# Attention scores one pair ahead, feed-forward pieces in traced order, other buffers for the first raw weights

## The chip, the cores and the metric

The kernel runs on one core of one Trainium2 chip. The metric is the time of one execution on the device in microseconds, as the median of several runs.

## What is computed

One layer of an encoder over two groups of tokens with the same weights: x_prompt (1024 tokens) and x_sample (512 tokens), width 1024, all float32. With DEPTH = 1 only the neighbourhood attention of the reference is used:

```python
def run(x):
    h = rms_norm(x, norm_mix[0])
    x = x + neighbourhood_attention(h, na_w_qkv[0], na_rpb[0], na_w_o[0])
    x = x + swiglu(rms_norm(x, norm_ffn[0]), ffn_w_gate[0], ffn_w_up[0], ffn_w_down[0])
    return rms_norm(x, norm_final)
```

Tokens lie on a grid 64 columns wide. There are 16 heads of width 64; 16 query columns look at a band of 32 key columns in 8 rows, with a learned bias and a mask. swiglu has a hidden width of 2816 and is (silu(x w_gate) * (x w_up)) w_down.

## The kernel before

A float32 product is made of three fp32r products on TensorE (PE): each operand is split into a high part (a CAST on ACT) and a low part (a subtraction on DVE, or for a few on POOL), and hi*hi, hi*lo and lo*hi are added up in PSUM. `split` (L139 to L145) does this for weights and activations.

The work comes in stages. (1) Norms, transposes and the V projection of all tokens (L250 to L324). (2) Attention of the prompt, by head pair hp = 0 to 7. A head pair has four steps (two halves g of the query rows, two pairs jj of column blocks), and `step` (L477) traces one: the scores of the pair's two blocks u = 0, 1 (`pss`, L397, with the bias addition and row maximum on DVE L405, Exp on ACT L408, reciprocal L410, scaling L412 on DVE for one head and L414 on ACT for the other), then the weighting (`po`, L434) and the collection (L444 to L447) of the pair before, then the flips, that is PE transposes (`ptt`, L423), of its own scores into `pT` (split on ACT L426, DVE L427). Between these stand fillers: `fill(part)` takes 6 matmuls (`pg`, L335) at a time of the q and k projection of the next head pair. Scores and flips take turns in four PSUM banks (tag "S"). (3) The same for the sample with two key tiles, beside the output projection (`pgo`, L593). (4) The feed-forward gate and up products, by Strassen's scheme of seven half-size products, for two chunks c of 768 tokens. `unit(c, p)` (L865) makes block p = 0 to 10 (256 columns) of gate and up: 14 products of 12 matmuls (L824), evicted by ACT (COPY, Silu) and DVE, followed by four sums on POOL (`gs`, L884 to L887) and seven stores of down operands to gop_d (L889). `w_ops` (L787) loads raw weights through `w_raw` (L779), whose counter `turn` deals them to two buffers of rpool and three of r2p (the right side of memory, where the attention's `wo` lay before), and splits them. (5) The down products (L1062).

Units of stage 4 take other work along: `tick` (L906) is called after each of the 14 products and takes one piece of a generator at every second call. In the first chunk, p = 1 to 10, these are the norm, transposes and operand sums of the second chunk (`pair1`, 42 pieces, three token groups); in the second chunk, p = 3 to 10, the sums of rows of w_down (`down_sums`, 56 pieces for 11 blocks, each with two subtractions on DVE L768, L770 and two on POOL L773, L775, two loads and two stores).

A scheduler sets the order in which each engine's instructions stand: it may move an instruction ahead of what was traced before it if no data forbids. Each engine and each DMA queue (SP's, ACT's, POOL's) then works strictly in that order. Only where the code records a manual dependency, as `in_order` (L98) does for the start, is the traced order kept.

## Time and profile before

| | |
|---|---|
| median of 3 runs | 1808.15 us (1807.66 to 1812.14) |
| the profiled execution | 1815.71 us, span 1813.8 us |
| PE busy | 1749.2 us (96%) |
| DVE busy | 1215.9 us (67%) |
| ACT busy | 870.6 us (48%) |
| POOL busy | 431.2 us (24%) |
| DMA engines, mean over the span | 163 GB/s |
| granted clock of TensorE, mean | 0.992 |

Busy time is the time in which an engine executes instructions; the rest of the span it waits or has nothing to do. PE is the engine that works nearly all the time, so the place of its waits matters, and what each of the other engines does just before.

### The profile page before, as it was taken

The numbers are of one execution on the slowest core, as the hardware profiler recorded it, in microseconds if no ns is written. First come the engines' busy times: TensorE is split into PE (matmuls) and PEld (weight loads), VectorE is DVE, ScalarE is ACT, GpSimd is POOL, SyncE is SP. The second block draws the span as 40 slices with busy tenths as digits, with TensorE's granted clock in tenths as the row PEclk, the third lists the DMA queues.
The fourth block names the chain that finished last, engine by engine and source line by source line (L and its number), as shares of the span: only waits on it lengthen the run. The fifth ranks groups of instructions, "written<-read, shape, count | busy, mean of one in ns | idle before, by whom it ended". The sixth has DMA issues, their size and how long they took to land.

```text
span 1813.8 us, 25894 instructions
## 1 busy us (share of the span) xinstructions
PE 1749.2 (96%) x9178; PEld 1527.3 (84%) x9178; DVE 1215.9 (67%) x2267; ACT 870.6 (48%) x1742; POOL 431.2 (24%) x509
## 2 busy tenths in 40 slices
PE   7999999999999999999999999989999999999998
PEld 6888777777777788779999999888999987888886
DVE  4401878788787666667877777988777756446553
ACT  4411777667785555544444445433344335433423
POOL 1111000000130000112424242565424352005300
PEclk9999999999999999999999999999999999999999
DMA  7755333333464453653553634888433269555633
GB/s 237 224 182 168 98 107 109 108 103 106 131 204 149 135 157 111 193 181 119 177 171 111 216 109 146 284 298 275 137 115 122 75 210 324 180 158 165 206 110 107
DMA packets 229858, 295.60 MB, mean 163 GB/s; under 512 B 27648, under 2 KB 173824, under 8 KB 229728
## 3 DMA queue, kind: packets, MB, share of 16 engines
q1 hardware_dynamic: 205744, 215.94, 39.3%
q0 software_dynamic: 21248, 69.62, 10.5%
q10 hardware_dynamic: 2736, 8.39, 1.5%
q8 instruction: 72, 1.18, 0.3%
q14 instruction: 58, 0.48, 0.1%
HBM read 218.45 MB, written 87.97 MB: 169 GB/s over the span
## 4 chain that ended last, share of the span: by engine, by line
PE 69%; DMA 11%; DVE 9%; ACT 4%; issue 4%; SPq 2%; POOL 2%; DVEq 0%; ACTq 0%; POOLq 0%
PE pa L824 16%; PE pd L1062 16%; PE pd L824 8%; PE pg L335 7%; PE pgv L281 7%; DMA vr<-v_d 5%; PE pgo L593 4%; PE pb L824 4%; PE pss L397 3%; SPq L381 2%; PE po L434 1%; PE ptt L423 1%; DMA gr<-gop_d 1%; DMA wt_d<-t 1%; ACT s L408 1%
## 5 line engine op out<-in xcount | busy, mean ns | idle before, releaser
L1062 PE MATMUL pd<-wd,go 128*128 128x512 f32 x1386 | 325.7, 396 | 3.6 <-DVE wd L142 2.6
L1062 PEld LDWEIGHTS pd<-wd,go 128*128 128x128 f32 x1386 | 260.4, 188 | 68.8 <-DVE wd L142 4.9
L824 PE MATMUL pa<-h,ws 128*128 128x384 f32 x1056 | 199.4, 336 | 8.7 <-ACT c L849 7.2
L335 PE MATMUL pg<-hTp,whl 128*128 128x512 f32 x768 | 201.9, 407 | 0.0
L824 PE MATMUL pd<-h,ws 128*128 128x384 f32 x1056 | 197.6, 334 | 0.0
L824 PEld LDWEIGHTS pa<-h,ws 128*128 128x128 f32 x1056 | 183.1, 188 | 12.0 <-ACT c L849 9.2
L824 PEld LDWEIGHTS pd<-h,ws 128*128 128x128 f32 x1056 | 184.3, 188 | 0.0
L142 DVE TENSOR_TENSOR ws<-wt,ws 128x1024 fp32r<-128x1024 f32 x88 | 109.9, 1250 | 90.9 <-ACT ws L141 90.9
L335 PEld LDWEIGHTS pg<-hTp,whl 128*128 128x128 f32 x768 | 139.2, 190 | 34.2 <-issue 7.7
L824 PE MATMUL pa<-h,wa 128*128 128x384 f32 x792 | 151.1, 343 | 8.3 <-DVE c L856 8.3
L824 PEld LDWEIGHTS pa<-h,wa 128*128 128x128 f32 x792 | 141.4, 191 | 10.5 <-DVE c L856 10.5
L593 PE MATMUL pgo<-wo,oh 128*128 128x512 f32 x576 | 139.0, 392 | 1.4 <-DVE oh L142 1.4
L141 ACT CAST go<-gr 128x768 fp32r<-128x768 f32 x84 | 65.7, 782 | 151.6 <-PE pd L1062 106.7
L408 ACT ACTIVATE s<-s,mx 128x384 f32<-128x384 f32 (+1 forms) x192 | 109.1, 570 | 54.8 <-DVE mx L405 54.8
L142 DVE TENSOR_TENSOR wa<-wr,wa 128x512 fp32r<-128x512 f32 x132 | 124.0, 952 | 13.1 <-ACT wa L141 12.1
L142 DVE TENSOR_TENSOR go<-gr,go 128x768 fp32r<-128x768 f32 x84 | 81.6, 972 | 75.0 <-ACT go L141 73.4
L593 PEld LDWEIGHTS pgo<-wo,oh 128*128 128x128 f32 x576 | 107.4, 188 | 24.4 <-DVE oh L142 1.8
L889 POOL DMA_DIRECT2D gop_d<-c x66 | 50.6, 766 | 313.1 <-DVE c L880 313.1
L141 ACT CAST wa<-wr 128x512 fp32r<-128x512 f32 x132 | 81.8, 621 | 88.5 <-PE pb L824 43.5
L141 ACT CAST ws<-wt 128x1024 fp32r<-128x1024 f32 x88 | 92.4, 1051 | 63.3 <-issue 49.7
L335 PE MATMUL pg<-hTs,whl 128*128 128x512 f32 x384 | 105.7, 411 | 2.0 <-DVE q L346 2.0
L824 PE MATMUL pb<-h,wa 128*128 128x384 f32 x528 | 101.0, 339 | 4.3 <-ACT wa L141 4.1
(158 smaller groups left out, 2945.3 us busy)
## 6 DMA issues: line engine op xcount, KB each, us to landing
wr<-ffn_w_gate SPq DMA_DIRECT2D x44, 512.0 KB
wr<-ffn_w_up SPq DMA_DIRECT2D x44, 512.0 KB
wr<-na_w_qkv SPq DMA_DIRECT2D x38, 512.0 KB
gop_d<-gs POOLq DMA_DIRECT2D x88, 192.0 KB, 5.7
gr<-gop_d SPq DMA_DIRECT2D x42, 384.0 KB
gr<-gop_d SPq DMA_DIRECT2D x42, 320.0 KB
gop_d<-c POOLq DMA_DIRECT2D x66, 192.0 KB, 2.5
vr<-v_d SPq DMA_DIRECT2D x192, 64.0 KB
```

Source lines behind the costliest of these rows:

```text
L141: nc.scalar.copy(hi, raw)
L142: nc.vector.tensor_tensor(lo, raw, f32(hi), ALU.subtract)
L281: nc.tensor.matmul(pg, hh[a][:, k, c:c + P], wv[k // 2][b][:, k % 2], start=(k == 0 and i == 0), stop=(k == KB - 1 and i == 2))
L335: nc.tensor.matmul(pg, w[:, a, k, :], h[b][:, k, c:c + 512], start=(k == 0 and i == 0), stop=(k == KB - 1 and i == 2))
L381: nc.sync.dma_start(out=raw[:, j * P:(j + 1) * P], in_=src[:, BS[j]:BS[j] + 32, :])
L397: nc.tensor.matmul(pt[:, :n], q[h * HD:(h + 1) * HD, a, j].rearrange("p r i -> p (r i)"), kv[:, krow:krow + nrow, BS[j]:BS[j] + 32], start ...
L408: nc.scalar.activation(s[:, :n], s[:, :n], AF.Exp, bias=mx, scale=-1.0, accum_out=sm)
L423: nc.tensor.transpose(pt[:, c * P:(c + 1) * P], s[:, c * P:(c + 1) * P], ident)
L593: nc.tensor.matmul(pg, ohs[k // 4][:, a, k % 4], wo[:, b, k, n * 512:(n + 1) * 512], start=(k == 0 and i == 0), stop=(k == KB - 1 and i == 2))
L824: nc.tensor.matmul(bank[:, :HT], a(y, k), b[:, z, k], start=start and k == 0 and i == 0, stop=k == KB // 2 - 1 and i == 2, skip_group_chec ...
L889: nc.gpsimd.dma_start(out=gop_d[i, 3 * c:3 * c + 3, :, p].rearrange("j q t -> q j t"), in_=a.rearrange("q (j t) -> q j t", j=3))
L1062: nc.tensor.matmul(pd, go[:, y, i - a], wds[m, i][:, z], start=(i == 0 and k == 0), stop=(i == NP - 1 and k == 2))
```

## The change

Four edits. In attention, `step` keeps the softmax tiles `ss` of the pair instead of its flipped `pT`, and flips them in the next step, ahead of their weighting; `fill` is called four times with one piece each; the tiles s have six buffers instead of four, tmp and oT one instead of two. In the feed-forward stage a piece's instructions on ACT, DVE, POOL and SP are chained in the order in which they are traced, behind the last instruction traced before it on the same engine (`pinned`). The counter `turn` starts at 4, so the first two raw halves go to rpool and the next three to r2p. The tile `edge`, at the very end of memory, has 224 bytes a partition instead of 96, which moves all pools of the right side by 128 bytes, to addresses that are multiples of 256; those of the left side in stages 2 to 4 already are.

```diff
-        edge = es.enter_context(tc.tile_pool(name="edge", bufs=1, side="right")).tile([P, 24], F32, name="edge")
+        edge = es.enter_context(tc.tile_pool(name="edge", bufs=1, side="right")).tile([P, 56], F32, name="edge")
...
+        def pinned(work, *engines):
+
+            traced = nc.cur_bb.bb.instructions
+            mark = traced[-1]
+            done = next(work, 0) == 0
+            start = next(k for k in reversed(range(len(traced))) if traced[k] is mark) + 1
+            for e in engines:
+                own = [i for i in traced[start:] if i.engine == e.engine]
+                if own:
+                    last = next((i for i in reversed(traced[:start]) if i.engine == e.engine), None)
+                    for a, b in zip([last] + own, own):
+                        if a is not None:
+                            tc.add_manual_dep(b, a.name, mybir.DependencyInfo(
+                                mybir.DependencyClass.NoSync, mybir.DependencyReason.DATA), reason="pinned")
+            return done
...
-                s = ap.tile([P, 384], F32, tag="s", name="s", bufs=4)
+                s = ap.tile([P, 384], F32, tag="s", name="s", bufs=6)
...
         def collect(pos, dst):
+            tmp = ap.tile([P, 2, P], F32, tag="tmp", name="tmp", bufs=1)
             for h in range(2):
...
-                tmp = ap.tile([P, 2, P], F32, tag="tmp", name="tmp")
...
-            oT = ap.tile([P, 512], F32, tag="o", name="oT", bufs=2)
+            oT = ap.tile([P, 512], F32, tag="o", name="oT", bufs=1)
...
             fill(0)
             if prev:
-                p, pT = prev.pop()
+                p, pss = prev.pop()
+                pT = []
+                for u, x in enumerate(pss):
+                    pT.append(flip(x, p["n"]))
+                    fill(1 + u)
                 pos = [psum("V", "po") for _ in range(2)]
                 for u in range(2):
                     weighted(pT[u], [x() for x in p["v"]], p["jj"] * 2 + u, p["n"], pos, u)
                 collect(pos, p["dst"])
                 if p["done"]:
                     p["done"]()
-            pT = []
-            for u, x in enumerate(ss):
-                pT.append(flip(x, st["n"]))
-                fill(1 + u)
+            else:
+                fill(1)
+                fill(2)
+            fill(3)
             if st:
-                prev.append((st, pT))
+                prev.append((st, ss))
...
-                run(fillers, 1 if part or last else 2)
+                run(fillers, 0 if last and part % 2 else 1)
...
-                run(fillers, 1 if part else 2)
-                run(ofill, 1 if part else 2)
+                run(fillers, 1)
+                run(ofill, 1)
...
-        turn = [0]
+        turn = [4]
...
-                    next(work, None)
+                    pinned(work, nc.scalar, nc.vector, nc.gpsimd, nc.sync)
```

Line numbers in the rows below are those of each kernel; up to 20 lines lie between the two (L405 before is L421 after, L773 is L793).

Place 1, a step of the prompt's attention on DVE (s: softmax tile, mx: row maximum, ri: reciprocal of the row sum, pT: flipped tile, tmp and oT: collected output). Before:

```order
L405 ISA s,mx<-pss,bp 128x384
L405 ISA mx 128x1
L410 RECIPROCAL ri<-sm 128x1
L405 ISA s,mx<-pss,bp 128x384
L405 ISA mx 128x1
L412 TENSOR_SCALAR s<-s,ri 128x384
L410 RECIPROCAL ri<-sm 128x1 x2
L412 TENSOR_SCALAR s<-s,ri 128x384
L410 RECIPROCAL ri<-sm 128x1
L445 TENSOR_TENSOR tmp<-tmp,po 64x256 x2
L447 TENSOR_TENSOR oT<-tmp,po 64x2x8x16 x2
L427 TENSOR_TENSOR pT<-ptt,pT 128x3x128 x4
```

and after:

```order
L421 ISA s,mx<-pss,bp 128x384
L421 ISA mx 128x1
L426 RECIPROCAL ri<-sm 128x1
L421 ISA s,mx<-pss,bp 128x384
L421 ISA mx 128x1
L428 TENSOR_SCALAR s<-s,ri 128x384
L426 RECIPROCAL ri<-sm 128x1 x2
L428 TENSOR_SCALAR s<-s,ri 128x384
L426 RECIPROCAL ri<-sm 128x1
L443 TENSOR_TENSOR pT<-ptt,pT 128x3x128 x4
L461 TENSOR_TENSOR tmp<-tmp,po 64x256
L463 TENSOR_TENSOR oT<-tmp,po 64x2x8x16
```

The four subtractions of pT stood behind the collection and belonged to the scores above them; now they stand ahead of the collection and belong to the pair before, which is the pair that is collected.

Place 2, ACT at the change from attention's output to unit 0 of the first chunk (oh: output operand, wa and ws: split weights, wr: raw weights, t<-x_d: loads for the second chunk's norm). Before:

```order
L141 CAST oh<-wr 128x512
L141 CAST wa<-wr 128x512
L676 DMA t_9327<-x_d 128x1024
L676 DMA t_9328<-x_d 128x1024
L141 CAST wa<-wr 128x512 x2
L842 COPY c<-pa 128x384
L680 ACTIVATE t_9325,ms<-t_9327 128x1024
L141 CAST wa<-wr 128x512
L141 CAST ws<-wt 128x1024 x2
L141 CAST wa<-wr 128x512 x2
```

and after:

```order
L157 CAST oh<-wr 128x512
L157 CAST wa<-wr 128x512 x2
L157 CAST ws<-wt 128x1024 x2
L157 CAST wa<-wr 128x512 x2
L862 COPY c<-pa 128x384
L157 CAST wa<-wr 128x512
L896 ACT_TABLE_LOAD
L896 ACTIVATE c<-c 128x384
```

All splits of the first gate block but its last stand ahead of the first eviction now, and the first norm loads of the second chunk have gone some 15 rows down.

Place 3, POOL in the second chunk (t: sums of rows of w_down, gs: sums of a unit, gop_d: stores of a unit). Before:

```order
L889 DMA gop_d<-gs 128x3x128 x4
L773 TENSOR_TENSOR t_13224<-t_13224,t_13223 128x512
L775 TENSOR_TENSOR t_13224<-t_13224 128x512
L773 TENSOR_TENSOR t_13448<-t_13448,t_13447 128x512
L775 TENSOR_TENSOR t_13448<-t_13448 128x512
L773 TENSOR_TENSOR t_13638<-t_13638,t_13637 128x512
L775 TENSOR_TENSOR t_13638<-t_13638 128x512
L889 DMA gop_d<-c 128x3x128 x2
L884 TENSOR_TENSOR gs<-c 128x384
```

and after:

```order
L909 DMA gop_d<-gs 128x3x128 x4
L795 TENSOR_TENSOR t_13176<-t_13176 128x512
L793 TENSOR_TENSOR t_13400<-t_13400,t_13399 128x512
L795 TENSOR_TENSOR t_13400<-t_13400 128x512
L909 DMA gop_d<-c 128x3x128 x2
L904 TENSOR_TENSOR gs<-c 128x384
L905 TENSOR_TENSOR gs<-gs,c 128x384
L906 TENSOR_TENSOR gs<-c 128x384
L907 TENSOR_TENSOR gs<-c,gs 128x384
L909 DMA gop_d<-c 128x3x128
L909 DMA gop_d<-gs 128x3x128 x4
L793 TENSOR_TENSOR t_13590<-t_13590,t_13589 128x512
```

Before, two or three row blocks of the sums stand between the sums of two units, and all 11 are done in the first units of the chunk; now one or two stand there, spread over eight units to the chunk's last.

## Rows read from the trace of the kernel before

**Rows 1.** The page, engines: busy time, share of the span, instructions.

```profile
PE 1749.2 (96%) x9178; PEld 1527.3 (84%) x9178; DVE 1215.9 (67%) x2267; ACT 870.6 (48%) x1742; POOL 431.2 (24%) x509
```

**Rows 2.** Waits of PE from 230 to 580: total us, times, longest.

```profile
PE pss L397 <- DVE pT L427: 5.5, 7, 0.9
PE ptt L423 <- ACT s L414: 5.2, 12, 1.4
PE ptt L423 <- DVE s L412: 4.8, 5, 1.4
PE pg L335 <- DVE q L346: 2.0, 1, 2.0
```

**Rows 3.** Timeline of PE, one head pair: start, duration, instructions [idle before].

```profile
330.80 2.19 PE L397 MATMUL pss<-kp,q 64*128 64x384 f32 x12 [0.86 <-DVE pT L427]
...
352.54 1.52 PE L397 MATMUL pss<-kp,q 64*128 64x384 f32 x12
...
373.66 1.37 PE L397 MATMUL pss<-kp,q 64*128 64x384 f32 x7 [0.84 <-DVE pT L427]
```

**Rows 4.** Windows: length, busy PE, PEld, DVE, ACT, POOL, clock, DMA, GB/s.

```profile
300.00:400.00 100.00, 95.86 (x561) 76.97 (x560) 78.57 (x228) 69.44 (x173) 7.58 (x19) 1.00 0.35 102
```

**Rows 5.** Windows of units: 0; 1 to 6; 11 to 14; 16 to 20.

```profile
797.40:833.50 36.10, 31.82 (x170) 30.99 (x169) 25.14 (x39) 20.30 (x31) 3.20 (x5) 0.91 0.55 176
833.50:1018.80 185.30, 181.37 (x1057) 179.98 (x1057) 145.78 (x199) 82.61 (x134) 65.46 (x70) 1.00 0.53 166
...
1136.10:1271.80 135.70, 122.63 (x673) 119.21 (x672) 122.37 (x143) 50.65 (x84) 78.80 (x66) 0.98 0.84 286
...
1301.50:1448.00 146.50, 146.50 (x842) 146.14 (x842) 107.47 (x141) 60.72 (x100) 52.41 (x55) 1.00 0.35 109
```

**Rows 6.** Timelines of SP, ACT and PE at the start of unit 0.

```profile
785.61 0.38 SPq L784 DMA_DIRECT2D wr<-ffn_w_gate  x1
...
797.64 0.38 SPq L784 DMA_DIRECT2D wr<-ffn_w_gate  x1
...
803.06 1.14 ACT L141 CAST wa<-wr 128x512 fp32r<-128x512 f32 x2 [17.93 <-DMA wr<-ffn_w_gate]
...
803.74 1.01 PE L824 MATMUL pb<-h,wa 128*128 128x384 f32 x2 [4.06 <-ACT wa L141]
```

**Rows 7.** Windows of low granted clock (seventh value), as in rows 4.

```profile
801.70:808.60 6.90, 4.65 (x13) 4.14 (x14) 4.97 (x8) 4.74 (x8) 0.00 (x0) 0.51 1.04 356
1235.20:1238.70 3.50, 3.50 (x11) 3.50 (x12) 3.50 (x6) 0.00 (x0) 0.78 (x1) 0.51 0.97 341
```

**Rows 8.** Timelines of PE, DVE and POOL in the second chunk.

```profile
1178.76 2.38 PE L824 MATMUL pa<-h,ws 128*128 128x384 f32 x12 [2.03 <-ACT c L849]
...
1178.91 2.89 DVE L768 TENSOR_TENSOR t<-t 128x512 f32<-128x512 f32 x1
...
1179.95 1.30 POOL L773 TENSOR_TENSOR t<-t,t 128x512 f32<-128x512 f32 x1
...
1192.98 0.69 DVE L768 TENSOR_TENSOR t<-t 128x512 f32<-128x512 f32 x1 [1.43 <-DMA t<-ffn_w_down]
```

**Rows 9.** Waits of PE from 800 to 1130, first chunk.

```profile
PE pa L824 <- ACT c L849: 3.9, 2, 2.4
```

**Rows 10.** Timelines of SP and PE at the start of the down stage.

```profile
1464.95 0.34 SPq L1000 DMA_DIRECT2D gr<-gop_d  x1
...
1481.02 5.34 PE L1062 MATMUL pd<-wd,go 128*128 128x512 f32 x14 [2.38 <-DVE wd L142]
```

**Rows 11.** Groups by shape: count, busy us, mean ns, idle before.

```profile
L335 PE MATMUL pg<-hTp,whl 128*128 128x512 f32 x768 | 201.9, 407 | 0.0
...
L335 PE MATMUL pg<-hTs,whl 128*128 128x512 f32 x384 | 105.7, 411 | 2.0 <-DVE q L346 2.0
```

**Rows 12.** Groups by shape, DVE: the bias addition and its maximum.

```profile
L405 DVE CUSTOM_DVE_ANT_0 s<-pss,bp 128x384 f32<-128x384 f32 x128 | 65.4, 547 | 1.2 <-PE pss L397 1.1
...
L405 DVE DVE_READ_ACCUMULATOR2_ANT mx<- 128x1 f32 x192 | 15.8, 83 | 0.0
```

## The prediction

> **What bounds the kernel now.** I read the shares of the engines first: PE is busy 1749.2 us of the span, 96% [rows 1], so a gain can only come out of PE's waits, of stretches in which its clock is low, and of waits too short for the list. Then the waits of PE by stage, and for the feed-forward stage the windows unit by unit, because there each unit holds the same work (14 products of 12 matmuls) and its length can be compared.
>
> Attention of the prompt: in 350 us PE waits 17.5 us for four things [rows 2], nearly all of it at two places of a step: the first scores (pss) wait for a score bank that the last split of a pT must free, and the flips (ptt) wait for the softmax (s, from ACT L414 or DVE L412). In the timeline of one head pair the step takes 42.86 us from scores to scores (330.80 to 373.66); the scores that start after a wait take 2.19 us and the unhindered ones 1.52 [rows 3]. DVE is not far behind PE there: 78.6 of 100 us [rows 4].
>
> Feed-forward: five units without extra pieces take 146.5 us, so 29.3 each, with PE never idle, although POOL works 52.4 us beside DVE in them [rows 5]. Unit 0 takes 36.1, the six units with the norm pieces 185.3 (9.5 more than six times 29.3), and the first four units of the second chunk 135.7 (18.5 more than 117.2). That last stretch is also where DVE is busy 122.4 of 135.7. These 34.8 us are the larger part of what can be had.
>
> **The change, part by part.**
>
> *First raw weights.* Unit 0's second raw half is loaded only at 797.64 [rows 6], after the last pgo (797.4, where the first window of rows 5 begins): its buffer lies where wo still was. ACT waits 17.93 us for it, and PE stands 4.06 us before the second product [rows 6]. The granted clock is then low (0.51, the 1.2 GHz level) from 801.7 to 808.6 [rows 7]. With the new start of the counter both halves of w_gate's first block go to rpool, whose second buffer could be loaded at 785.61 already [rows 6], some 12 us before it is needed; w_up's two halves then take the late place, and its first product comes seven products after 797.4, 14.6 us later by the unit's 29.3, against 5.4 us from issue (797.64) to ACT (803.06) [rows 6]. In the new order ACT splits both before the first COPY (place 2 of the order). So the unit loses its 6.8 us of excess; I take 6.3. Ends: 4.1 if the clock still falls, 6.8 if all goes, and nothing if a load meets another wait.
>
> *Pieces in traced order.* 56 pieces of down_sums stood, by the scheduler's choice, in the first four units of the second chunk; now 7 stand in each of eight units, p = 3 to 10 (place 3 of the order). The work stays. What is saved is the crowding: in those units a subtraction of DVE takes 2.89 us while POOL runs its own, and 0.69 alone, and PE waits 2.03 us for a COPY that ACT has queued behind a Silu that waits for DVE [rows 8]. Price of a piece in uncrowded units: the 42 norm pieces cost 9.5 us, 0.23 each, PE's own transposes in that; their named PE waits alone are 3.9 us [rows 9], 0.09 each. So 56 pieces cost 5.2 to 12.9 us; I take 7, nearer the lower end because these pieces put nothing on PE or ACT, and leave 1 us for the operand reloads, which stay in the first unit (my choice). Gain 18.5 - 7 - 1 = 10.5; ends 5 and 13.
>
> Here a rule speaks against it. The row shows the price of meeting: 2.89 for 0.69 [rows 8]. The Trainium skill (SBUF — State Buffer, section on the two separate sides) says that DVE with two SBUF inputs and GpSimd take a shared port pair as an exclusive lock, held for the whole instruction, the other blocking fully. By that rule spreading saves nothing of the blocked time. What speaks for my value without it: the five clean units, where POOL's 52.4 us beside DVE cost PE nothing [rows 5], so blocked time counts only where DVE has no slack. It is a rival below.
>
> The norm pieces of the first chunk are pinned too. They stood near their traced places already, the first token group of the three about a unit earlier. Of their 9.5 us the 3.9 of waits [rows 9] could go, or as much could come back if a DMA issue in ACT's queue waits for its buffer; I take 1 gained. Pinned DMA issues of SP: the raw weights' loads are queued behind the stores of the sums (which wait for POOL), but come some 12 us early, as above. One of them is exposed: the loads of the down stage now stand behind the last store of the sums. They started at 1464.95, when hx came free, and PE waited 2.38 us at 1481.02 for the first split [rows 10]; the last sums now fall into that very unit. The last of them on POOL is traced behind the unit's twelfth product, at 1448.0 + 12 x 2.09 = 1473, so the loads could come up to 8 us later, of which the split's own place behind the unit's end hides most. I take 2 us lost; ends 0 and 8.
>
> *Scores a pair ahead.* A step now issues its scores, then flips the pair before, and weights it at once (place 1 of the order). PE's matmuls are the same number. The flips' softmax was finished a step ago, and the bank that the next scores want was freed by flips with 24 matmuls between. So of [rows 2] the 5.5 us go, with the 0.67 us (2.19 - 1.52) that hung on the block behind, for seven head-pair changes 4.7; the waits of flips for s (5.2 + 4.8 = 10.0) would go too, but flips now wait for banks that the new scores fill, until DVE has added the bias. I let half of the 10.0 stay, and 4.2 us come new at head-pair changes, where the raw splits stand in DVE's queue before the bias additions. Gain 5.5 + 4.7 + 5.0 - 4.2 = 11. Ends: 23 if everything of these goes, and a loss, priced as a rival. Eight s tiles would be live at once, and six buffers hold them: the third bias addition of a step waits for the first flip. The single oT is stored by POOL after a step and written again one step later, 10.7 us (a quarter of 42.86), which hides the store. The extra step at the end is filled with output projection.
>
> *Right side by 256 bytes.* pg with its operand on the right side (hTp) takes 407 ns, on the left (hTs, already at a multiple) 411 [rows 11]. I take 0; ends -1 and +1 us, for loads, which are prefetched.
>
> **Sum.** 6.3 + 10.5 + 1 - 2 + 11 + 0 = 26.8 us. Against the profiled execution's 1815.7 us that is 1788.9; that execution is 7.6 us above the median of the runs (1808.15, of 1807.66 to 1812.14), so the median becomes 1781.
>
> **Rivals.**
> - *Attention frees nothing*: DVE's queue, not the order, is the limit (78.6 of 100 us [rows 4], and its queue is in order, mixed with ACT's). For: flips already wait mostly for DVE's and ACT's chain. Against: PE's waits there sit at two fixed places. Time 1781 + 11 = 1792.
> - *The lock total stays*: the sums cost the same wherever they stand, and only the low clock goes, 3.5 us at half speed [rows 7], twice in these units (their mean clock is 0.98 [rows 5]), so 3.5 us gained in place of 10.5: 1788.
> - *All of it goes*: 6.8 + 13 + 3.9 + 0 + 23 = 46.7 us off the median, so 1761.
> - *Slower*: in each of the 32 prompt steps the second pair's flips wait for both bias additions of that pair, because these wait in turn for the first pair's flips (six buffers): 2 x (547 + 83) ns = 1.26 us [rows 12], 40.3 us in all, against 17.5 us that go. Attention then loses 22.8 in place of winning 11: 1781 + 11 + 22.8 = 1815. It decides from (26.8 - 11 + 17.5) / 32 = 1.04 us a step; I think it unlikely because a projection of six matmuls lies between the two flips.
> - *The change does not do what it says*: excluded for the places shown, as the order of the built program has moved as described; what runs can still show is that no wait stood there. That is the first two rivals together, 1781 + 11 + 7 = 1799.
>
> **How the numbers follow.** Forecast 0.50 (its own range 1773 to 1789), attention frees nothing 0.17, lock total 0.12, both 0.05, all goes 0.10, slower 0.06. A difference of 0.3% (5.4 us) is about what a measurement of this kernel can tell from none. Range 1764 to 1799: it holds the first four cases and leaves out the slower one and most of the one in which all goes. Faster is all but the slower case and some loss I have not thought of: 0.91; same 0.04; slower 0.05.
>
> **What would show it.** Right: no PE wait and full clock at the start of unit 0; units 0 to 3 of the second chunk near 29.3 to 31 us, with units 4 to 10 a few tenths longer than 29.3; pss no longer in PE's list of waits for pT; ptt waiting for DVE's bias addition, by tenths. Wrong: units of the second chunk at 31 us each through to the end (the lock), a head pair still at 42 us (attention), flips waiting over 1 us in each step (slower), or a first split of the down stage that PE awaits for 5 us or more.

## The result, and the profile after

| | before | after |
|---|---|---|
| median | 1809.84 us (1807.66 to 1812.14, 6 runs) | 1800.32 us (1796.30 to 1802.49, 6 runs) |
| ratio | | 0.9941, 95% interval 0.9924 to 0.9959 |
| span of the profiled execution | 1813.8 us | 1799.2 us |

The change makes the kernel faster by 0.6%, some 10 us. The forecast was 27 us and 1781, with a range of 1764 to 1799: the sign was right, and the time lies just above the range. The two profiled executions are 14.6 us apart, more than the medians, because that of before lies some 6 us above its median.

Where the time went is read from the lengths of the stages, each from the first matmul of its kind in the trace to the first of the next (us; the sample's attention ends at its last scores, the down products at their last matmul):

| stage | before | after | difference | forecast |
|---|---|---|---|---|
| norms and V projection | 181.1 | 182.1 | +1.1 | 0 |
| attention of the prompt | 338.2 | 338.6 | +0.5 | -11 |
| attention of the sample | 196.8 | 205.8 | +9.0 | 0 |
| rest of the output projection | 81.3 | 83.8 | +2.5 | 0 |
| feed-forward, 22 units | 680.7 | 661.6 | -19.1 | -17.8 |
| down products | 328.6 | 320.1 | -8.5 | +2 |

Each column is one execution, and the attention's lengths vary between executions. Nine traces of this study run attention in the old order (before, e1, e2, e3, e5, e6, e10, e11 and e13, all described below): the prompt takes 334.9 to 340.8 us in them, on average 336.8, and the sample 196.8 to 202.7, on average 199.8. Four run the prompt in the new order (after, e4, e8, e14), in 338.6 to 340.7, on average 339.7; three of them also the sample, in 205.8 to 208.1, on average 206.8. So the new order costs some 3 us in the prompt, 7 in the sample and 3 in the rest of the output projection, and the column before has the shortest sample of the nine.

So the feed-forward stage did what was forecast, the attention did the opposite, and the down products gave 8.5 us that the forecast did not have.

The page of the changed kernel, engines (busy time, share of the span, instructions):

```profile
PE 1738.5 (97%) x9178; PEld 1514.6 (84%) x9178; DVE 1219.1 (68%) x2267; ACT 868.4 (48%) x1742; POOL 435.8 (24%) x509
```

Against [rows 1] PE has the same 9178 matmuls in 10.7 us less busy time. The windows of units 0, 1 to 6, 11 to 14 and 16 to 20 of the changed kernel, and its attention of the sample as the last line (length; busy PE, PEld, DVE, ACT, POOL; clock; DMA share; GB/s):

```profile
810.41:840.40 29.99, 29.47 (x170) 29.15 (x169) 19.79 (x30) 13.95 (x22) 2.10 (x3) 1.00 0.51 159
840.40:1022.90 182.50, 180.61 (x1057) 179.58 (x1056) 138.81 (x198) 84.93 (x138) 73.83 (x72) 1.00 0.51 160
1140.40:1259.60 119.20, 117.41 (x674) 116.31 (x673) 94.72 (x124) 51.44 (x84) 46.58 (x46) 1.00 0.50 167
1289.30:1440.30 151.00, 147.28 (x841) 145.38 (x841) 128.66 (x155) 60.28 (x100) 76.20 (x70) 1.00 0.59 203
...
520.78:726.80 206.02, 192.77 (x1014) 152.08 (x1013) 135.22 (x393) 112.09 (x295) 22.71 (x23) 0.98 0.45 139
```

The first four answer to [rows 5]: unit 0 falls from 36.1 to 30.0 at full clock, the crowded four units from 135.7 to 119.2, and the units that were clean take 151.0 in place of 146.5, because they carry the pieces now.

Waits of PE in the changed kernel from 230 to 580 (total us, times, longest), which answer to [rows 2]:

```profile
PE ptt L439 <- DVE mx L421: 10.2, 23, 0.8
PE po L450 <- DVE pT L443: 4.4, 9, 1.8
PE pg L351 <- DVE whl L158: 2.3, 2, 1.9
PE pss L413 <- ACT ks L368: 0.7, 1, 0.7
```

and from 580 to 813, with the sample's attention and the output projection:

```profile
PE pss L413 <- ACT ks L368: 3.1, 1, 3.1
PE po L450 <- DVE pT L443: 2.8, 4, 1.1
PE pg L351 <- DVE q L362: 2.5, 1, 2.5
PE pgo L613 <- DVE oh L158: 1.3, 1, 1.3
```

The scores no longer wait for pT, as meant. But in this window, which holds 61 us of the sample, flips wait as long for the bias additions (10.2 us) as they did for the softmax (5.2 + 4.8), and the weighting, which waited for nothing before, now waits for pT. In the sample the weighting waits for pT too, and the scores once for ks, 3.1 us in place of 0.8 and 0.9; q and oh were waited for before as well (2.0 us in [rows 2], and 1.4). The wait for ks is not tied to the new order: e17 below, in the old one, has it with 3.4 us. A head pair of the prompt takes 42.5 us from scores to scores (42.86 in [rows 3]):

```profile
326.40 1.34 PE L413 MATMUL pss<-kp,q 64*128 64x384 f32 x12
...
368.91 1.34 PE L413 MATMUL pss<-kp,q 64*128 64x384 f32 x12
```

The prompt's attention can also be divided by the starts of PE's matmuls, each counted to the start of the next, so that also waits too short for the list are in it (a wait counts with the matmul ahead of it, that of a flip mostly with the projection pg):

| us in the prompt | pss | ptt | pg | po |
|---|---|---|---|---|
| before | 56.5 | 46.8 | 189.4 | 45.5 |
| after | 44.7 | 43.8 | 198.2 | 52.0 |

The scores give 11.8 us, and the projection and the weighting take 8.8 and 6.5 back.

The start of the down stage, against [rows 10]: the wait for the first split is the same as before.

```profile
1474.86 5.60 PE L1082 MATMUL pd<-wd,go 128*128 128x512 f32 x11 [2.35 <-DVE wd L158]
```

### The profile page after: what moved, and what is told of

The parts are those of the page before. It is cut to its first block, busy times and chain, and to the rows that moved or that the text cites. A ratio compares the mean times of both kernels' runs of the same rounds, so it can differ in the third digit from the quotient of the medians.

```text
span 1799.2 us, 25883 instructions
## 1 busy us (share of the span) xinstructions
PE 1738.5 (97%) x9178; PEld 1514.6 (84%) x9178; DVE 1219.1 (68%) x2267; ACT 868.4 (48%) x1742; POOL 435.8 (24%) x509
## 4 chain that ended last, share of the span: by engine, by line
PE 54%; DVE 8%; DMA 5%; issue 3%; ACT 2%; POOL 1%; SPq 1%; POOLq 0%; DVEq 0%; ACTq 0%
PE pd L1082 17%; PE pa L844 17%; PE pd L844 8%; PE pb L844 4%; PE pgo L613 4%; DMA vr<-v_d 2%; PE pg L351 2%; PE po L450 1%; SPq L397 1%; DMA wr<-ffn_w_up 1%; PE pss L413 1%; DMA gop_d<-c 1%; DMA xo<-x_prompt 0%; DVE c L900 0%; DVE ws L158 0%
## 5 line engine op out<-in xcount | busy, mean ns | idle before, releaser
L1082 PE MATMUL pd<-wd,go 128*128 128x512 f32 x1386 | 317.6, 391 | 3.2 <-DVE wd L158 2.3
L351 PE MATMUL pg<-hTp,whl 128*128 128x512 f32 x768 | 206.6, 404 | 0.0
L158 DVE TENSOR_TENSOR ws<-wt,ws 128x1024 fp32r<-128x1024 f32 x88 | 118.6, 1349 | 83.9 <-ACT ws L157 83.9
L844 PE MATMUL pa<-h,wa 128*128 128x384 f32 x792 | 145.9, 335 | 1.8 <-DVE c L876 1.8
L844 PEld LDWEIGHTS pa<-h,wa 128*128 128x128 f32 x792 | 137.6, 188 | 2.9 <-DVE c L876 2.8
L158 DVE TENSOR_TENSOR wa<-wr,wa 128x512 fp32r<-128x512 f32 x132 | 112.5, 864 | 18.7 <-ACT wa L157 17.5
L351 PE MATMUL pg<-hTs,whl 128*128 128x512 f32 x384 | 111.2, 419 | 4.8 <-DVE q L362 2.5
L443 DVE TENSOR_TENSOR pT<-ptt,pT 128x384 fp32r<-128x384 f32 (+1 forms) x192 | 90.9, 506 | 17.7 <-ACT pT L442 16.4
```

The costliest lines, as they stand in the source:

```text
L158: nc.vector.tensor_tensor(lo, raw, f32(hi), ALU.subtract)
L351: nc.tensor.matmul(pg, w[:, a, k, :], h[b][:, k, c:c + 512], start=(k == 0 and i == 0), stop=(k == KB - 1 and i == 2))
L443: nc.vector.tensor_tensor(pT[:, :n, 1], pv, f32(pT[:, :n, 0]), ALU.subtract)
L844: nc.tensor.matmul(bank[:, :HT], a(y, k), b[:, z, k], start=start and k == 0 and i == 0, stop=k == KB // 2 - 1 and i == 2, skip_group_chec ...
L1082: nc.tensor.matmul(pd, go[:, y, i - a], wds[m, i][:, z], start=(i == 0 and k == 0), stop=(i == NP - 1 and k == 2))
```

## Experiments

### Each part alone

Four runs, each the kernel before with one part of the change. The edits are the hunks of the diff above:

```diff
e1   the tile edge: P, 24 -> P, 56
e2   turn = [0] -> turn = [4]
e3   next(work, None) -> pinned(work, nc.scalar, nc.vector, nc.gpsimd, nc.sync)
e4   step, fill, collect and the buffers of s, tmp and oT
```

> Theory (addresses count): the two traces differ in the down products, 328.6 to 320.1 us, where a matmul of 512 columns now starts every 227 ns in place of 229 to 238, and in the V projection, 231 to 235 ns, the wrong way. With the addresses alone the down stage is then 320 to 322 us, the V projection 1 to 2 us longer, the second chunk's products with wa from the right side 1 to 2 us shorter in all: 6 to 8 us less than before in the whole, ratio 0.996. Rival (the down stage is quicker because its loads and stores were moved by the pinned pieces): the down stage stays at 328 us and the time within 1 us of before.

> Theory (as predicted): unit 0 takes 29.3 to 30.5 us in place of 36.1, with no wait of 4 us at its second product and full granted clock; 6 us less in the whole, ratio 0.9967. Rival (the wait moves to w_up's first halves or the clock falls all the same): unit 0 over 32 us, gain under 4 us.

> Theory (spreading takes the crowding out): units 11 to 14 take 119 to 121 us in place of 135.7, units 15 to 20 some 180 in place of 176.2, units 1 to 6 some 182.5 in place of 185.3, the wait ahead of the first down product stays near 2.4 us; 12 to 14 us less in the whole, ratio 0.993. Rival (part of what the feed-forward stage lost came from the aligned addresses of hx, the raw and the split weights, not from the order): 8 to 10 us less.

> Theory (the order costs what it gains): in the prompt's attention the scores lose their waits but the weighting, now right behind its flips, waits for the split of pT, so its length stays within 2 us of 338; in the sample's, where the scores hardly waited, only the new waits remain and it is 8 to 12 us longer; the whole 8 to 13 us slower, ratio 1.006. Rival (the order gains as forecast and the aligned addresses of hTp, wo and oh cost it): 8 to 11 us faster. Second rival (neither): within 3 us.

| part alone | ratio | 95% interval | of 1809.84 us |
|---|---|---|---|
| e1, addresses | 0.9964 | 0.9949 to 0.9978 | -6.5 |
| e2, first raw weights | 0.9969 | 0.9958 to 0.9979 | -5.6 |
| e3, pinned pieces | 0.9936 | 0.9924 to 0.9949 | -11.6 |
| e4, scores ahead | 1.0081 | 1.0068 to 1.0094 | +14.7 |

They add up to -9.0 us, against -9.5 by the medians and -10.7 by the ratio for the change: the parts hardly touch each other. Three gain and one takes back more than half.

*e1.* The down stage is 320.7 us with the addresses alone, so the gain there has nothing to do with the pinned loads. The down matmuls by tile (count, shortest, median and longest duration in ns), before and in e1:

```profile
L1062 PE MATMUL pd<-wd,go x1386: 387/392/797, 1478.1 to 1806.3; 128*128 128x512 f32 x198
```

```profile
L1062 PE MATMUL pd<-wd,go x1386: 387/389/796, 1477.2 to 1797.5; 128*128 128x512 f32 x198
```

and the same window of 280 us, before and in e1:

```profile
1500.00:1780.00 280.00, 279.81 (x1203) 225.38 (x1203) 156.40 (x212) 111.48 (x186) 51.36 (x54) 1.00 0.58 186
```

```profile
1500.00:1780.00 280.00, 279.68 (x1233) 231.04 (x1232) 159.26 (x216) 114.41 (x192) 51.49 (x54) 1.00 0.59 189
```

PE is hardly idle in either and the clock is full; it just gets through 1233 matmuls in place of 1203, 227 ns apart in place of 233.

*e2.* Unit 0 takes 31.0 us with no wait at its second product; one of 1.4 us for ACT's COPY stands ahead of its fifth:

```profile
801.48:832.50 31.02, 29.66 (x169) 29.07 (x168) 19.69 (x32) 17.72 (x28) 4.58 (x5) 1.00 0.56 187
```

*e3.* Units 11 to 14 take what they take in the changed kernel, with POOL's work in them down from 78.8 to 46.6 us ([rows 5]):

```profile
1129.30:1248.50 119.20, 118.04 (x674) 116.86 (x673) 93.51 (x123) 51.43 (x84) 46.59 (x46) 1.00 0.50 168
```

Over the whole second chunk it is 332.1 us in place of 342.0. The 11.6 us lie between the theory's 12 to 14 and the rival's 8 to 10, and the interval reaches into both; the lengths of the units are the theory's, with the old addresses.

*e4.* The prompt's attention takes 340.2 us, the sample's 206.5 and the rest of the output projection 84.7. The loss is there with the old addresses too, so it is the order's; the first rival is out.

### The three that gain, together, and one more address

e5 is the changed kernel with attention as before. In e6 the V projection's weights move by 128 bytes as well:

```diff
-            fill = vp.tile([P, 480], F32, tag="fill", name="fill", bufs=1)
+            fill = vp.tile([P, 512], F32, tag="fill", name="fill", bufs=1)[:, :480]
```

> The three parts that gained when alone, together, attention as before. Theory (the parts are separate and add up): 0.9964 x 0.9969 x 0.9936 = 0.987 of before. Rival (the parts share a gain, or the time comes back elsewhere): above 0.990.

> As the run with the three parts, and the weights of the V projection moved by 128 bytes. Theory (what costs PE is that the two operands of a product lie at different places modulo 256 bytes): all 576 products of the V projection start about 227 ns apart and it takes 4 to 5 us less than with the three parts alone, 0.984 to 0.985 of before. Rival (the V projection is set by the loads and splits of its operands, not by PE's reads): less than 1 us.

e5 measured 0.9874 (0.9857 to 0.9890), the product of the three is 0.9870. e6 measured 0.9851 (0.9833 to 0.9868), medians of 1788.56 and 1783.43 us in the same comparison. The V projection fell from 181.3 to 179.0 us, half of what was expected: by the starts of its matmuls it keeps the pace now (226.7 ns apart in its later part), but in the first 60 us PE waits 9.7 us for the norm all the same (9.6 in e5). The intervals of the two overlap; the stage's length and the medians agree in the sign.

### Which addresses matter

e10 has the right side at 64 modulo 256, e11 the right side as before (128) and the V projection's weights at 0. One execution each (1823.06 and 1814.04 us against 1813.60 for the kernel before), of which only the stages are read.

```diff
e10  the tile edge: P, 24 -> P, 40
e11  the tile fill: P, 480 -> P, 512, as in e6
```

> Before, with the right side at 64 modulo 256. Theory (only equal places modulo 256 bytes let PE run undisturbed): the down matmuls, whose one operand lies on the left at 0, still start every 229 to 238 ns, and the stage takes 327 to 329 us. Rival (a quarter of the line is enough apart from a half): 227 ns and 320 to 322 us.

> Before, with the V projection's weights moved to 0 modulo 256 and the right side left at 128. Theory (the difference of the two operands' places counts): its 192 products with hTs (at 0) start every 226.7 ns, its 384 with hTp (at 128) on average 230 to 236. Rival (the place of the streamed weights alone counts): 226.7 ns in both.

In e10 the down stage took 328.5 us, as before: 64 bytes apart is no better than 128. The V projection of e11, by tile, where hTp lies at 128, hTs at 0 and the weights at 0:

```profile
L281 PE MATMUL pgv<-wv,hTp x384: 388/393/796, 10.4 to 135.7; 128*128 128x512 f32 x192
L281 PE MATMUL pgv<-wv,hTs x192: 387/389/476, 66.4 to 157.5; 128*128 128x512 f32 x192
```

and before, with hTp and the weights at 128 and hTs at 0:

```profile
L281 PE MATMUL pgv<-wv,hTp x384: 387/389/797, 10.6 to 135.4; 128*128 128x512 f32 x192
L281 PE MATMUL pgv<-wv,hTs x192: 387/393/479, 66.8 to 157.7; 128*128 128x512 f32 x192
```

The short median stands where the two operands have the same place modulo 256 (128 and 128, or 0 and 0), the long one where the places differ, and crossing the weights swaps the two lines. So it is the difference that counts, not a multiple as such; differences of 0, 64 and 128 bytes were run. (The projections within the attention do not show it: their median is 393 to 395 ns with whl at 0 and hTp at 128 before, or at 0 after. Why is open.) The change equalised the down products and made the V projection's hTp unequal, its +1.1 us.

### What the attention waits for

e7 moves the step's fourth filler between flips and weighting; e8 uses the new order in the prompt alone; e9 takes turns (all parts of the change, and e6's edit). All three are against the kernel before.

```diff
e7 (beside e4)
+                fill(3)
                 pos = [psum("V", "po") for _ in range(2)]
...
-            fill(3)
e8 (beside e4; the sample's part of it)
-                step(st, fill)
+                step(st, fill, False)
e9 (beside after; the loop in step)
...
+            for u in range(2):
+                if st:
+                    next(sc[u])
+                    ss.append(next(sc[u]))
+                fill(2 * u)
+                if p:
+                    pT.append(flip(pss[u], p["n"]))
+                fill(2 * u + 1)
...
```

> As the run with the scores alone, but the step's fourth filler stands between the flips and the weighting. Theory (the weighting waits for the split of pT that stands right ahead of it): the excess of po over 120 ns a matmul in the prompt, some 8 us with the scores alone, falls to 2 or 3, and the prompt's attention to 333 to 337 us; the whole some 1.004 of before. Rival (the flips' waits for banks set the step): the prompt's attention stays at 340 us, the waits move to pss.

> Scores a pair ahead in the prompt alone, the sample's attention in the order of before. Theory (the sample's attention and the output projection carry most of the loss): sample 197 to 200 us and output projection 81 to 82, the whole 2 to 5 us slower than before, ratio 1.002. Rival (the loss comes from the changeover of the prompt's end): ratio 1.005 to 1.008 as with the whole part.

> All parts of the change and the moved weights of the V projection, but a step takes turns: scores of one block, flips of the block of the pair before, scores of the other block, its flips, with a filler behind each, then the weighting. Theory (the flips and scores wait because both blocks' scores and both blocks' flips swing the four score banks as a whole, so that each needs what was issued one filler ago): with turns each needs a bank that was used two fillers and another product earlier; PE's listed waits in the prompt's attention fall from 13 to under 5 us, its length from 340 to 325 to 332 us, against 335 in the order of before; with the sample's attention near 200 us the whole is 0.978 to 0.983 of before. Rival (DVE's and ACT's work is the limit, not the banks): the prompt's attention stays at 335 to 340 us, the whole at 0.986 to 0.992.

*e7: 1.0145 (1.0125 to 1.0165).* My theory fell, and so did its rival. The weighting hardly waits any more, as expected, but the prompt's attention takes 357.5 us, and now the flips wait:

```profile
PE ptt L423 <- DVE mx L405: 30.2, 25, 3.4
PE po L434 <- DVE pT L427: 0.8, 1, 0.8
```

Some 3 us of it come once per head pair. DVE and ACT around one such wait (PE's flip starts at 292.82 after 2.94 us):

```profile
289.26 1.23 DVE L145 SCALAR_TENSOR_TENSOR whl<-wr,whl 128x1024 fp32r<-128x1024 f32 x1 [2.18 <-ACT whl L144]
290.40 0.86 DVE L445 TENSOR_TENSOR tmp<-tmp,po 64x256 f32<-64x256 f32 x2
291.30 0.87 DVE L447 TENSOR_TENSOR oT<-tmp,po 64x256 f32<-64x256 f32 x2
292.19 0.56 DVE L405 CUSTOM_DVE_ANT_0 s<-pss,bp 128x384 f32<-128x384 f32 x1
```

```profile
288.17 1.06 ACT L144 ACTIVATE whl<-wr 128x1024 fp32r<-128x1024 f32 x1 [1.93 <-DMA wr<-na_w_qkv]
```

A raw weight arrives late; its split stands in the queues of ACT and DVE ahead of the bias additions; the flips need these to free their banks. The sample tells another story: its attention takes 198.5 us in e7 against 206.5 in e4, from which it differs only by the place of that filler. So at least there the weighting right behind its flips carried the loss, as far as one execution of each can show.

*e8: 1.0061 (1.0048 to 1.0074)*, not 1.002 but inside the rival's 1.005 to 1.008: by the ratios the new order in the prompt alone costs 11.0 us of e4's 14.7, though the two intervals overlap. The rest of the output projection is back at 81.3 us, the prompt takes 340.7, and the sample's attention 203.4, a little above the 196.8 to 202.7 of the old order that it has here. Its largest wait stands at the first changeover of head pairs: PE's scores stand 3.3 us for ks, and ACT has

```profile
595.25 0.62 ACT L141 CAST v<-vr 128x512 fp32r<-128x512 f32 x1 [5.64 <-DMA vr<-v_d]
595.78 0.64 ACT L426 CAST pT<-ptt 128x256 fp32r<-128x256 f32 x2
596.30 0.60 ACT L352 CAST ks<-pg 128x512 fp32r<-128x512 f32 x1
```

a split of raw V that waits for its load, and the eviction of ks behind it: the same pattern. How the loss is shared between the prompt's steps and what they leave for the sample stays open: by its stages e8's attention is 7.5 us above the average of the old order, of which 3.9 lie in the prompt.

*e9: 0.9978 (0.9968 to 0.9988)*, worse than the changed kernel and than the rival said (335 to 340 us, 0.986 to 0.992): the prompt's attention takes 358.2 us.

```profile
PE po L450 <- DVE pT L443: 16.8, 12, 2.9
PE pss L413 <- DVE mx L421: 2.7, 2, 2.4
```

Again it comes once per head pair, and again behind a split of raw V that waits for its load (ACT):

```profile
373.90 0.62 ACT L157 CAST v<-vr 128x512 fp32r<-128x512 f32 x1 [2.90 <-DMA vr<-v_d]
```

The waits cost more than their length. The prompt's attention has a mean granted clock of 0.95 here, which is some 18 us of 358 at the 2.4 GHz level lost to seven stretches at 1.2 GHz, each right behind one of these waits:

```profile
178.70:536.90 358.20, 338.12 (x1865) 263.50 (x1865) 280.05 (x775) 243.66 (x590) 27.72 (x63) 0.95 0.37 107
236.00:246.00 10.00, 7.26 (x35) 5.51 (x35) 7.49 (x17) 6.41 (x15) 0.30 (x1) 0.83 0.41 114
```

### The raw splits moved out of the way

First I dealt the six loads and splits of a head pair out evenly, 2, 1, 2, 1 a step in place of 2, 1, 1, 2 (1, 2, 1, 2 in e15):

```diff
-                        if i in (0, 1, 2, 5, 6, 7) or last:
+                        if i in (0, 1, 2, 4, 5, 6) or last:
```

> As the run that takes turns, with the six loads and splits of a head pair dealt out as 2, 1, 2, 1 to its four steps in place of 2, 1, 1, 2. Theory (the raw splits in DVE's and ACT's queues wait for their loads and hold up the splits of pT): the wait of 2.2 to 2.9 us once per head pair, and the low clock behind it, go; the prompt's attention falls from 358 to 330 to 338 us, the whole from 0.998 to 0.980 to 0.987 of before. Rival (DVE's own work, whatever its order): the prompt's attention stays above 350.

> As the quickest so far (three parts and the moved weights, attention in the order of before), with the same spread of loads and splits. Theory (there the waits for loads are hidden by the flips that stand far behind): prompt 333 to 337 us, the whole within 0.15% of 0.985. Rival (they cost there too): prompt under 331.

> As the run with the scores alone, with the same spread. Theory (splits): the waits of flips for the bias addition fall from 9 to under 5 us in the prompt, its length from 340 to 333 to 337. Rival (banks): the waits and the length stay within 2 us.

> As the run that takes turns, with 1, 2, 1, 2 splits a step. Theory (splits): the prompt's attention 330 to 340 us, as with 2, 1, 2, 1. Rival (DVE's work): above 350.

They measured 0.9996 (0.9985 to 1.0006), 0.9860 (0.9835 to 0.9884), 1.0071 (1.0051 to 1.0090) and 0.9985 (0.9974 to 0.9996), as e9, e6, e4 and e9 did, and for a plain reason: the scheduler had set the same instructions in the same order on every engine. The edit changed the code and not the program, so these four tell nothing of the question. They serve as repeats: one program came out at 0.9978, 0.9996 and 0.9985, so two ratios of different comparisons can be 0.2% apart.

Then the splits were pinned as the change pins its pieces, behind what is traced ahead of them on ACT and DVE, that is behind the collection of their step. These three runs also keep the deal of 2, 1, 2, 1 from above, which the pin makes effective; the pin with the old deal was not run. e18 lacks the moved weights of e6, which e16 and e17 have:

```diff
-                            chores.do()
+                            pinned(chores.one(), nc.scalar, nc.vector)
...
+            def one(self):
+                self.do()
+                yield
```

> As the run that takes turns, with the raw splits of V and of the projection weights pinned behind the collection of their step on ACT and DVE. Theory (the splits, waiting for loads ahead of the splits of pT, cost the new order): po's wait of 2 to 3 us once per head pair goes, with the low clock behind it; the prompt's attention falls from 358 to 328 to 338 us, the whole to 0.978 to 0.986 of before. Rival (banks or DVE's work): above 350 us, the whole above 0.993.

> As the quickest so far (attention in the order of before), with the same pinned splits. Theory: in the old order the flips stand behind all of it, and the waits for s (5 to 10 us) lose the share that came from a split ahead of the scaling: prompt 328 to 335 us, the whole 0.980 to 0.986. Rival (the pinned splits now hold up the bias additions of the next step): prompt above 337, the whole above 0.987.

> The changed kernel with the same pinned splits. Theory (splits): its prompt's attention falls from 339 to 330 to 335 us, the whole from 0.994 to 0.988 to 0.992. Rival (banks: the flips stand one filler behind the scores whose banks they need): within 0.15% of 0.994, and the flips' waits for the bias additions stay at 8 to 10 us.

| attention in | without the pin | with it | to the first feed-forward matmul, without | with |
|---|---|---|---|---|
| turns (e9, e16) | 0.9978 | 0.9879 (0.9860 to 0.9898) | 819.3 us | 795.2 us |
| the changed order (after, e18) | 0.9941 | 0.9898 (0.9878 to 0.9917) | 810.4 | 798.1 |
| the old order (e6, e17) | 0.9851 | 0.9838 (0.9819 to 0.9858) | 796.7 | 786.9 |

By the ratios, of 1809.84 us, the pin is worth 17.9 us with turns, 7.8 in the changed order and 2.4 in the old one, where the intervals overlap. With turns the waits all but vanish and the clock is back at 0.99; the prompt's attention is as the theory had it, the whole a little above its 0.978 to 0.986. Windows of the prompt's attention in e16, e18 and e17:

```profile
178.40:506.60 328.20, 324.10 (x1859) 253.21 (x1859) 279.71 (x772) 242.08 (x586) 26.93 (x62) 0.99 0.39 116
```

```profile
181.10:509.00 327.90, 319.10 (x1858) 248.41 (x1858) 275.11 (x772) 236.63 (x587) 29.18 (x62) 0.99 0.39 115
```

```profile
179.30:503.20 323.90, 315.08 (x1862) 254.57 (x1862) 274.95 (x777) 241.78 (x589) 29.04 (x62) 0.99 0.39 116
```

(7 to 12 projection matmuls, under 3 us, have moved from each window into the sample.) So the place of the raw splits is shown to cost in both new orders: up to the first feed-forward matmul the pin is worth 24.1 us with turns and 12.3 in the changed kernel. The old order gains 9.8 us there in these traces, though the profiled execution of e6 lies 3.8 us above its median. What the new order loses against the old is 11.1 us from the first scores to the first feed-forward matmul without the pin (628.3 in the changed kernel, 617.2 in e5) and 9.3 with it (616.9 in e18, 607.6 in e17); by the ratios it is 12.1 and, less 4.2 us for the moved weights that e18 lacks, 6.7. So the splits explain a part of the loss, and the greater part stays. In e18 the waits that are listed in the prompt are

```profile
PE ptt L443 <- DVE mx L425: 7.4, 16, 3.4
```

against 7.8 us in e17 (3.0 + 2.5 for s, 2.3 for pT). In the starts of its matmuls po takes 53.8 us in e18 and 48.8 in e17, and the projection's matmuls, behind which the short waits of the flips lie, 186.3 against 180.3; the scores and flips give back 6.8 of these 11. But that the waits of po are the rest of the loss is not shown. e16 has them no more (po 49.5 us) and few waits of flips (3.1 us in the list), and its prompt takes 328.2 us all the same: there the scores need 55.6 us in place of e17's 48.0. Each new order is slow at another product, and what sets its pace stays open. In the sample's attention and the rest of the output projection e18 is 3.9 and 1.4 us longer than e17; pinning the sample's splits was not tried.

e17 is the quickest kernel of the study, 1779.35 us (1777.39 to 1780.57) against 1806.63 for the kernel before in the same comparison. It beats both kernels clearly, e6 only by its median (1783.43, and 1786.28 in the repeat).

## Why the prediction was right and wrong

- **First raw weights, 6.3.** Right: 5.6 us alone, unit 0 at 30.0 in the changed kernel, no wait at its second product, full clock.
- **Pieces in traced order, 10.5 and 1.** Right, in size and place: the second chunk went from 342.0 to 331.6 us, units 1 to 6 from 185.3 to 182.5; alone the pin gives 11.6. The rival that the lock total stays is out as a time (3.5 us in these units), but its total did stay. The Trainium skill (SBUF — State Buffer, section on the two separate sides) says that a DVE instruction with two SBUF inputs and a GpSimd instruction that reads SBUF block each other for the whole instruction; by that alone spreading would have saved none of the blocked time. The trace agrees: over the second chunk DVE is busy 266.1 us before and 267.3 after with the same work, POOL 153.5 and 154.6.

```profile
1136.10:1478.10 342.00, 328.26 (x1849) 324.08 (x1847) 266.11 (x330) 133.47 (x222) 153.53 (x145) 0.99 0.55 184
```

```profile
1140.40:1472.00 331.60, 323.63 (x1849) 319.68 (x1847) 267.30 (x331) 133.52 (x222) 154.59 (x145) 1.00 0.55 188
```

The two subtractions of the sums got shorter, and other instructions took the meetings over, the split of ws most of all. Before and after:

```profile
L142 DVE TENSOR_TENSOR ws<-wt,ws 128x1024 fp32r<-128x1024 f32 x43 | 53.3, 1240 | 41.5 <-ACT ws L141 41.4
...
L770 DVE TENSOR_TENSOR t<-t,t 128x512 f32<-128x512 f32 x11 | 12.0, 1093 | 1.7 <-DMA t<-ffn_w_down 1.6
...
L768 DVE TENSOR_TENSOR t<-t 128x512 f32<-128x512 f32 x11 | 10.6, 960 | 8.2 <-issue 6.8 <-DMA t<-ffn_w_down 1.4
```

```profile
L158 DVE TENSOR_TENSOR ws<-wt,ws 128x1024 fp32r<-128x1024 f32 x43 | 61.7, 1435 | 47.0 <-ACT ws L157 47.0
...
L788 DVE TENSOR_TENSOR t<-t 128x512 f32<-128x512 f32 x11 | 8.6, 786 | 0.0
...
L790 DVE TENSOR_TENSOR t<-t,t 128x512 f32<-128x512 f32 x11 | 7.5, 683 | 0.0
```

What went is PE's idle time, from 13.7 to 8.0 us, and the low clock that [rows 7] show at 1235.2 and that came once more at 1269.4, some 3.4 us of work in all. The same blocked time cost PE where it was crowded, and little where it was spread, as the prediction argued for its value.

- **Start of the down stage, -2.** The wait I feared did not come (2.35 us against 2.38); 2 us too many taken off.
- **Right side by 256 bytes, 0 with ends -1 and +1.** Wrong by its own step: I compared the attention's projections at two places (407 and 411 ns, [rows 11]), which of all products do not show the effect, and asked for the place of one operand alone. What counts is the difference between the two operands' places; I had not looked at the down products, whose operands lay 128 apart. Measured 6.5 us; that is luck, and without it the change would be worth some 3 us.
- **Scores a pair ahead, +11 with a loss as rival.** This is the step that failed: alone it costs 14.7 us, 25.7 from the forecast. The scores did what was forecast, 11.8 us less from start to start in the prompt against 5.5 + 4.7. Three other terms were wrong. "Weights it at once" was put at nothing and is a new wait: the split of pT now lies between flips and weighting (po waits 4.4 us in the list, and takes 6.5 us more from start to start in the prompt). The flips were to give 0.8 us (10.0 gone, 5.0 and 4.2 new), but [rows 2] run from 230 to 580 and the sample begins at 519.24: in the prompt alone the flips waited 6.4 us before and wait 10.7 now (lines below), and with the projection they take 5.8 us more from start to start. And the sample's sixteen steps were not priced at all: there, where the scores hardly waited, little was to be gained, and with the rest of the output projection 9.0 + 2.5 us were lost (7 and 3 on the average of the traces). The upper end of 23 us also adds up to only 22.2 from its rows (17.5 + 4.7). Of the causes of the loss one is shown, the place of the raw splits, and it is a part; the rest stays open. Waits of flips in the prompt, before (181 to 519) and after (182 to 521):

```profile
PE ptt L423 <- ACT s L414: 5.4, 13, 1.4
PE ptt L423 <- DVE s L412: 1.0, 2, 0.8
```

```profile
PE ptt L439 <- DVE mx L421: 10.3, 23, 0.8
...
PE ptt L439 <- DVE ri L426: 0.4, 1, 0.4
```

- **The rivals.** By the number the first two rivals together (1799) came nearest to 1800.3, by chance: the lock's part of it did not come. "Attention frees nothing" has the sign wrong too, since the prompt loses some 3 us. The slower rival named the right wait, flips behind bias additions, but through the buffers of s; e7 shows it through splits of raw tiles in an in-order queue.

The sum with the measured parts is 6.5 + 5.6 + 11.6 - 14.7 = 9.0 us.

## What to carry to other kernels

When a step is turned round, list for every product what it waited for before and what it will stand behind now, for all the stages that run the step, and price the product that waited for nothing. A split or cast that waits for a load should stand behind the urgent work of its step in an in-order queue; pinning it there was worth 18 and 8 us in the two new orders (2 in the old one, within the noise), while moving it in the code did nothing, since the scheduler put it back. Compare the addresses of a matmul's two operands: if they differ modulo 256 bytes, a pad of some bytes may give 2 to 3% of the time of such matmuls (227 against 233 ns here).

## What the runs showed of the hardware that I had not expected

The pace of fp32r matmuls of 512 columns depends on where their two operands lie relative to each other: 227 ns from start to start when both are at the same place modulo 256 bytes (0 and 0), 229 to 238 when they lie 64 or 128 apart, with PE busy throughout and the clock at its 2.4 GHz level. Over 1386 down matmuls that is 8 us. The Trainium skill (TensorE: Matmul & The Clock Gate, step by step of a matmul) says that PE reads its two operands through two independent ports, and that loading the next weights takes no read bandwidth from the running matmul. The runs show what the page does not speak of, that the places of the two operands count together: the medians by tile are 389 ns with equal places and 392 to 395 with unequal ones, outside the attention, and the order swaps when one operand is moved. Whether it is the loading of weights that holds the reads up is not shown.

A wait of PE of 2 to 3 us costs about twice its length where the granted clock falls behind it: the prompt's attention in e9 had 19.5 us of listed waits for pT and the bias additions, and lost up to some 18 more to the 1.2 GHz level.
